# The last layer of a filter network on halves of TensorE's rows, two channel groups at a time

## The chip, the cores and the metric

The kernel runs on one core of a Trainium2 chip. The metric is the device time of one execution in microseconds; the median of several runs counts. An execution of the kernel before is shown by a hardware profile, on whose rows the text rests.

## The reference, cut to what matters

The program computes two layers of a hybrid network for 128 context tokens and 1024 latent tokens. Layer 0 has a state-space mixer and a Hyena mixer side by side, layer 1 is neighbourhood attention. The Hyena mixer convolves each of 1024 channels with a long filter that a small network computes from positions. Only this network is touched by the change:

```python
hdn = jnp.sin(freq * (feats @ w1 + b1))
hdn = jnp.sin(freq * (hdn @ w2 + b2))        # (L, 64)
filt = (hdn @ w3).astype(f32)                # w3: (64, 2048)
decay = jnp.exp(-t * jnp.abs(deltas)[None])
h_fwd = filt[:, :D_B] * decay
h_bwd = filt[:, D_B:] * decay
return jnp.concatenate([h_fwd, jnp.zeros((1, D_B), f32), h_bwd[:0:-1]], axis=0)
```

The last product, `hdn @ w3`, contracts over 64 hidden units only. It is needed for two directions (forward and backward), for a length of 1024 and one of 128, and for 8 groups of 128 channels. Its result times the decay is the filter, which the kernel then carries into the frequency domain.

## The kernel before, in words

The kernel is written with tiles, for which a framework derives the semaphores. It gives out buffers, and decides the order of each engine's instructions when the program is built; on the chip each engine then takes its own queue in that order. In the trace it can be seen that this order follows the program's text where work is ready, and takes later work forward where it isn't.

The projections set the frame. `proj` (L150 to L168) computes one chunk of 128 output channels for 1152 tokens as three blocks of 384 columns, each 24 matmuls on TensorE: 8 pieces of the inner dimension by three products (L160, L161, L162). The three products come from splitting each operand into a high and a low float32r part, hi·hi, hi·lo and lo·hi. Blocks go to a PSUM pool of three banks (`pj`); ScalarE empties them. Weights come by SP's queue into `wraw` one chunk ahead (`w_load`, L119), ScalarE casts the high part (`whi`, L132) and VectorE subtracts the low part (`wlo`, L133).

Between blocks, `tick` (L92) lets background work take a step: a Python generator runs up to its next `yield`, and what it issues stands between two blocks in the program's text. In the stage `xbc` (12 chunks, three ticks each, of which the first two chunks were computed ahead into three `pj` and three background banks) the one background generator is `filter_groups` (L526 to L569), at one step a tick. All background work takes its PSUM from a second pool of five banks (`bg`, `ps()`, L79).

`filter_groups` walks over the 8 channel groups. For each group it needs the filter in time, F (128 partitions, 18 blocks of 128 channels: 8 forward, 8 backward, 2 for the short length), which `filter_time` (L488 to L524) makes. Then come the first stage of a transform on VectorE (`stage_a`, L419, which starts with L537), the matmuls of the short transform (L548, L550) and of the second stage (`stage_b`, L464, lines L471 to L480), copies by ScalarE into H, and a store of H by the POOL queue. `filter_time` of the next group is called between `stage_a` and `stage_b` of this one, so F has two buffers.

`filter_time` for one group does the following.

- It fills a tile w3 of 128 rows and 256 columns: rows 0 to 63 hold the forward weights in columns 0 to 127, rows 64 to 127 the backward weights in columns 128 to 255, and the other two quarters are set to zero on POOL (L496, L497). ScalarE casts the high part wh (L500) and VectorE subtracts the low part wl (L501).
- The hidden layer `hdn` (high `hh`, low `hl`) has 128 partitions: 64 hidden units at the forward positions, and 64 at the backward ones. With the zeros in w3, one matmul over 128 rows gives both directions side by side.
- For each of 9 blocks j of 128 positions it issues three matmuls (L514, L515, L516) of 256 columns. Two j share one PSUM bank.
- ScalarE computes the decay with four exponentials of 128 by 128 (L519) into dc, which has one buffer. VectorE multiplies bank and dc into F (L520), one instruction of 512 columns for two j. The bank is free then.
- At last VectorE adds the bias row to position 0 (L523). Decay rates and bias come in one broadcast load, dl.

Of the kernel before, what the change touches and what calls it, by code (L numbers as in the profile page):

```python
# [9 lines left out]
AF = mybir.ActivationFunctionType  # L10
ALU = mybir.AluOpType
# [32 lines left out]
def bc(ap, shape):  # L44
    return ap.to_broadcast(shape)


class Net:
# [330 lines left out]
    def filter_mlp(self, keep, pool, px):  # L379
# [6 lines left out]
        for h in range(2):  # L386
            self.dma(w2[64 * h:64 * h + 64], i["hw2"])
        ft = self.t(pool, [128, 2304], "F", bufs=2)[0:33]
        self.dma(ft, i["feats"])
# [98 lines left out]
    def filter_time(self, g, pool):  # L488

        nc = self.nc  # L490
        i = self.i

        w3 = self.t(pool, [128, 256], "w3")
        wh = self.t(pool, [128, 256], "w3h", F32R)
        wl = self.t(pool, [128, 256], "w3l", F32R)
        nc.gpsimd.memset(w3[0:64, 128:256], 0.0)  # L496
        nc.gpsimd.memset(w3[64:128, 0:128], 0.0)  # L497
        for h in range(2):
            self.dma(w3[64 * h:64 * h + 64, 128 * h:128 * h + 128], i["hw3"][:, g, h])
        nc.scalar.copy(wh, w3)  # L500
        nc.vector.tensor_tensor(out=wl, in0=w3, in1=wh.bitcast(F32), op=ALU.subtract)  # L501
        dl = self.t(pool, [128, 2, 128], "dl")
        self.dma(dl.rearrange("p a c -> p (a c)"), i["dlhb"][g:g + 1].to_broadcast([128, 256]))
        F = self.t(pool, [128, 18, 128], "F", bufs=2)
        Fj = F[:, 0:16].rearrange("p (d j) c -> p j d c", d=2)
        hh, hl = self.hdn
        for j0 in range(0, 9, 2):
            n = min(2, 9 - j0)
            p = self.ps()
            dc = self.t(pool, [128, 2, 2, 128], "dc")  # L510
            for j in range(j0, j0 + n):
                o = p[:, (j - j0) * 256:(j - j0) * 256 + 256]
                js = slice(j * 128, j * 128 + 128)
                nc.tensor.matmul(o, hh[:, js], wh, start=True, stop=False)  # L514
                nc.tensor.matmul(o, hl[:, js], wh, start=False, stop=False)  # L515
                nc.tensor.matmul(o, hh[:, js], wl, start=False, stop=True)  # L516
                for d in range(2):
                    n1 = 8 * d + j if j < 8 else 16 + d
                    nc.scalar.activation(dc[:, j - j0, d], dl[:, 0], AF.Exp, scale=self.tcol[:, n1:n1 + 1])  # L519
            nc.vector.tensor_tensor(out=Fj[:, j0:j0 + 2] if n == 2 else F[:, 16:18].unsqueeze(1),  # L520
                                    in0=p[:, :n * 256].rearrange("p (j d c) -> p j d c", j=n, d=2), in1=dc[:, :n], op=ALU.mult)

        nc.vector.tensor_tensor(out=F[0:1, 0:17:16], in0=F[0:1, 0:17:16], in1=bc(dl[0:1, 1:2], [1, 2, 128]), op=ALU.add)  # L523
        return F  # L524

    def filter_groups(self, pool):  # L526

        nc = self.nc
        V = nc.vector
        self.tcol = self.t(pool, [128, 18], "tcol")  # L530
        self.dma(self.tcol, self.i["tcol"])
        Fn = self.filter_time(0, pool)
        yield
        for g in range(8):
            F = Fn
            sm = self.t(pool, [128, 8, 128], "sm")
            V.tensor_tensor(out=sm, in0=F[:, 0:8], in1=F[:, 8:16], op=ALU.add)  # L537
            V.tensor_tensor(out=F[:, 0:8], in0=F[:, 0:8], in1=F[:, 8:16], op=ALU.subtract)
            A = self.t(pool, [128, 16, 128], "A")
            self.stage_a(sm, F[:, 0:8], F[:, 8:10], F[:, 10:12], A, pool, "u8")  # L540
            yield
            if g < 7:
                Fn = self.filter_time(g + 1, pool)
                yield
            H = self.t(pool, [128, 20, 128], "H")
            p = self.ps()
            for n in range(2):
                nc.tensor.matmul(p[:, 0:128], self.tcf[:, n, :], F[:, 16 + n], start=(n == 0), stop=(n == 1))  # L548
            for n in range(2):
                nc.tensor.matmul(p[:, 128:256], self.tcf[:, 2 + n, :], F[:, 16 + n], start=(n == 0), stop=(n == 1))  # L550
            nc.scalar.copy(H[:, 18:20], p[:, 0:256].rearrange("p (a c) -> p a c", c=128))
            nc.scalar.copy(H[:, 17], p[:, 0:128])
            for k2 in range(4):
                p = self.ps()
                for j in range(2):
                    self.stage_b(A, 2 * k2 + j, p[:, j * 128:(j + 1) * 128], p[:, 256 + j * 128:256 + (j + 1) * 128])
                nc.scalar.copy(H[:, 1 + 2 * k2:3 + 2 * k2], p[:, 0:256].rearrange("p (a c) -> p a c", c=128))
                nc.scalar.copy(H[:, 9 + 2 * k2:11 + 2 * k2], p[:, 256:512].rearrange("p (a c) -> p a c", c=128))
                if k2 == 0:
                    nc.scalar.copy(H[:, 0], p[:, 0:128])  # L560
                if k2 == 1:
                    yield

            for b, im in ((0, 9), (17, 19)):
                V.tensor_copy(H[0:1, b], H[0:1, im])
                V.memset(H[0:1, im], 0.0)
            self.store(self.Hd[g], H)
            yield
# [1273 lines left out]
```

## Time and profile before

| | us |
|---|---|
| three runs | 2075.86, 2077.14, 2079.71 |
| median | 2077.14 |
| the profiled execution's own time | 2079.07 |
| its span, from the first to the last instruction | 2077.3 |
| TensorE matmuls busy in it | 2019.4 |
| VectorE busy | 1313.7 |
| ScalarE busy | 917.9 |

In the profile PE is TensorE's matmul queue, PEld its weight loads, DVE VectorE, ACT ScalarE, POOL GpSimd and SP the queue that issues most transfers. A row of the timeline gives the start in us, the duration, the engine, the line of the kernel, the operation, the tiles (written <- read), the shape and how many instructions were put together (x2). A shape such as 64*128 means a matmul over 64 rows of the array and 128 columns of weights; 128x256 is what streams through. Matmuls overlap, so the cost of one in a queue is the distance between the starts of two, not its duration.

### The profile page before, as it was taken

The numbers are of one execution on the slowest core, as the hardware profiler recorded it, in microseconds if no ns is written. First come the engines' busy times: TensorE is split into PE (matmuls) and PEld (weight loads), VectorE is DVE, ScalarE is ACT, GpSimd is POOL, SyncE is SP. The second block draws the span as 40 slices with busy tenths as digits, with TensorE's granted clock in tenths as the row PEclk, the third lists the DMA queues.
The fourth block names the chain that finished last, engine by engine and source line by source line (L and its number), as shares of the span: only waits on it lengthen the run. The fifth ranks groups of instructions, "written<-read, shape, count | busy, mean of one in ns | idle before, by whom it ended". The sixth has DMA issues, their size and how long they took to land.

```text
span 2077.3 us, 33946 instructions
## 1 busy us (share of the span) xinstructions
PE 2019.4 (97%) x13088; PEld 1820.7 (88%) x13088; DVE 1313.7 (63%) x2720; ACT 917.9 (44%) x2100; POOL 110.5 (5%) x233
## 2 busy tenths in 40 slices
PE   5999999999999999999999999999999999999998
PEld 3999997889999999888888899998888888888877
DVE  6887745145778787898899774654444344454464
ACT  3676642263333322554466511535445454443232
POOL 0010001110000000000000000100000000000000
PEclk9999999999999999999999999999999999999999
DMA  8142349554222113433353351422333223333462
GB/s 340 47 150 93 107 166 295 206 181 163 80 74 72 65 58 102 152 120 127 117 180 109 129 167 41 120 81 86 95 115 88 78 79 97 111 117 123 129 212 82
DMA packets 114265, 257.13 MB, mean 124 GB/s; under 512 B 27031, under 2 KB 62487, under 8 KB 111639
## 3 DMA queue, kind: packets, MB, share of 16 engines
q1 hardware_dynamic: 98728, 191.87, 29.1%
q0 software_dynamic: 15376, 63.09, 8.3%
q8 instruction: 104, 1.70, 0.4%
q14 instruction: 57, 0.47, 0.1%
HBM read 187.10 MB, written 67.80 MB: 123 GB/s over the span
## 4 chain that ended last, share of the span: by engine, by line
PE 82%; DVE 7%; DMA 4%; ACT 3%; issue 3%; SPq 0%; POOL 0%; POOLq 0%; DVEq 0%; ACTq 0%
PE pj L160 15%; PE pj L161 15%; PE pj L162 15%; PE bg L1315 3%; PE bg L1327 3%; PE bg L1298 3%; PE pj L1155 2%; PE pj L1156 2%; PE pj L1157 2%; PE bg L778 1%; PE bg L777 1%; PE bg L915 1%; PE pj L1353 1%; PE bg L290 1%; PE pj L1354 1%
## 5 line engine op out<-in xcount | busy, mean ns | idle before, releaser
L160 PE MATMUL pj<-hh,whi 128*128 128x384 f32 x1728 | 601.1, 348 | 2.7 <-DVE acc L846 1.8
L161 PE MATMUL pj<-hl,whi 128*128 128x384 f32 x1728 | 586.4, 339 | 0.0
L162 PE MATMUL pj<-hh,wlo 128*128 128x384 f32 x1728 | 586.1, 340 | 0.0
L160 PEld LDWEIGHTS pj<-hh,whi 128*128 128x128 f32 x1728 | 324.7, 188 | 23.7 <-issue 18.0
L161 PEld LDWEIGHTS pj<-hl,whi 128*128 128x128 f32 x1728 | 324.9, 188 | 7.5 <-issue 6.6
L162 PEld LDWEIGHTS pj<-hh,wlo 128*128 128x128 f32 x1728 | 324.6, 188 | 5.5 <-issue 4.5
L133 DVE TENSOR_TENSOR wlo<-wraw,whi 128x1024 fp32r<-128x1024 f32 x108 | 131.7, 1221 | 156.0 <-ACT whi L132 153.3
L132 ACT CAST whi<-wraw 128x1024 fp32r<-128x1024 f32 x108 | 113.3, 1050 | 259.1 <-PE pj L161 229.6
L1233 DVE CUSTOM_DVE_ANT_0 sz<-bg,Tb 128x512 f32<-128x512 f32 x128 | 83.5, 688 | 127.3 <-PE bg L1298 126.7
L583 ACT COPY raw<-pj 128x384 f32<-128x384 f32 (+2 forms) x140 | 56.0, 402 | 171.2 <-PE pj L162 84.0
L1235 ACT ACTIVATE sz<-sz,mx 128x512 f32<-128x512 f32 x128 | 91.6, 717 | 54.0 <-DVE mx L1233 53.2
L160 PE MATMUL pj<-yhi,whi 128*128 128x384 f32 x324 | 111.4, 344 | 3.8 <-DVE x L1076 2.8
L162 PE MATMUL pj<-yhi,wlo 128*128 128x384 f32 x324 | 110.8, 342 | 0.0
L161 PE MATMUL pj<-ylo,whi 128*128 128x384 f32 x324 | 109.7, 339 | 0.0
L1329 ACT COPY Pt<-bg 128x512 f32<-128x512 f32 (+1 forms) x144 | 71.9, 548 | 32.1 <-PE bg L1327 28.3
L1155 PE MATMUL pj<-whi,hh 128*128 128x256 f32 x288 | 82.9, 289 | 0.0
L1156 PE MATMUL pj<-wlo,hh 128*128 128x256 f32 x288 | 80.8, 281 | 0.0
L1157 PE MATMUL pj<-whi,hl 128*128 128x256 f32 x288 | 80.5, 280 | 0.0
L1327 PE MATMUL bg<-csq,sz 128*128 128x128 f32 x528 | 73.9, 280 | 0.0
L908 ACT ACTIVATE xw<-xt,wd 128x64 f32<-128x64 f32 x256 | 64.6, 336 | 8.7 <-PE bg L915 8.1
L1327 PEld LDWEIGHTS bg<-csq,sz 128*128 128x128 f32 x528 | 56.7, 141 | 13.0 <-issue 12.7
L160 PEld LDWEIGHTS pj<-yhi,whi 128*128 128x128 f32 x324 | 61.4, 189 | 7.1 <-issue 5.5
(411 smaller groups left out, 4021.3 us busy)
## 6 DMA issues: line engine op xcount, KB each, us to landing
wraw<-in_we SPq DMA_DIRECT2D x52, 512.0 KB, 3.6
wa<-in_wada SPq DMA_DIRECT2D x32, 512.0 KB, 6.8
wraw<-in_wo SPq DMA_DIRECT2D x24, 512.0 KB, 3.6
Tb<-Cd SPq DMA_DIRECT2D x256, 48.0 KB, 2.0
Hd<-H POOLq DMA_DIRECT2D x8, 1280.0 KB, 5.4
H<-Hd SPq DMA_DIRECT2D x8, 1280.0 KB, 6.5
xt<-xtd SPq DMA_DIRECT2D x17, 512.0 KB, 4.5
wraw<-in_woe SPq DMA_DIRECT2D x16, 512.0 KB, 4.2
```

The costliest lines, as they stand in the source:

```text
L132: self.nc.scalar.copy(hi, r)
L133: self.nc.vector.tensor_tensor(out=lo, in0=r, in1=hi.bitcast(F32), op=ALU.subtract)
L160: nc.tensor.matmul(p[:, :NB], wh, xh[k][:, sl], start=(k == 0), stop=False)
L161: nc.tensor.matmul(p[:, :NB], wh, xl[k][:, sl], start=False, stop=False)
L162: nc.tensor.matmul(p[:, :NB], wl, xh[k][:, sl], start=False, stop=(k == nk - 1))
L1155: nc.tensor.matmul(p[:, :256], self.hh[k][:, ts], hi[:, q:q + 256], start=(k == 0), stop=False)
L1156: nc.tensor.matmul(p[:, :256], self.hh[k][:, ts], lo[:, q:q + 256], start=False, stop=False)
L1157: nc.tensor.matmul(p[:, :256], self.hl[k][:, ts], hi[:, q:q + 256], start=False, stop=(k == 7))
L1233: V.tensor_tensor_reduce(out=z[:, :n], in0=s, in1=tb, scale=-1.0, scalar=3.0e38, op0=ALU.add, op1=ALU.min, accum_out=m1)
L1235: nc.scalar.activation(z[:, :n], z[:, :n], AF.Exp, bias=m1, scale=-1.0, accum_out=sm)
L1327: nc.tensor.transpose(pt[:, b * 128:(b + 1) * 128], p[:, b * 128:(b + 1) * 128], self.ident)
L1329: nc.scalar.copy(t[:, :nb * 128], pt[:, :nb * 128])
```

## The change

`filter_time` makes two groups at a time, and the two directions are no longer held apart by zeros.

- w3 now holds, in rows 0 to 63, the forward weights of both groups side by side (256 columns), and in rows 64 to 127 the backward weights of both. There are no zeros, and no memsets.
- Each matmul over 128 rows becomes two over 64: rows 0 to 63 (forward) into one PSUM bank, rows 64 to 127 (backward) into another. The two stand next to each other in the text. The columns stay 256, but they are now two groups of one direction, where they were two directions of one group. So a pair of groups has 54 matmuls of half height, where two calls before had 54 of full height.
- A block of two j takes two banks of the five.
- The multiply into F is done for each group and direction by itself: four instructions of 256 columns for a block of two j and two groups, where there were two of 512. dc is taken once for each group.
- The decay rates come in two loads, one for each group, and the two bias rows in two loads into a tile hb, which shares w3's buffer.
- `filter_groups` calls it before group 0 and again in groups 1, 3 and 5, behind the short transform's matmuls, where both F tiles have been read. The calls of the other groups and their yields fall away, so the generator has 28 yields where it had 32.

```diff
-        w3 = self.t(pool, [128, 256], "w3")
+        w3 = self.t(pool, [128, 2, 128], "w3")
...
-        nc.gpsimd.memset(w3[0:64, 128:256], 0.0)
-        nc.gpsimd.memset(w3[64:128, 0:128], 0.0)
         for h in range(2):
-            self.dma(w3[64 * h:64 * h + 64, 128 * h:128 * h + 128], i["hw3"][:, g, h])
+            self.dma(w3[64 * h:64 * h + 64], i["hw3"][:, g:g + 2, h])
...
+        hb = self.t(pool, [128, 2, 128], "w3")
+        for m in range(2):
+            self.dma(dl[:, m], i["dlhb"][g + m:g + m + 1, 0:128].to_broadcast([128, 128]))
+            self.dma(hb[0:1, m], i["dlhb"][g + m:g + m + 1, 128:256])
+        Fs = [self.t(pool, [128, 18, 128], "F", bufs=2) for n in range(2)]
         hh, hl = self.hdn
+        R = (slice(0, 64), slice(64, 128))
         for j0 in range(0, 9, 2):
             n = min(2, 9 - j0)
-            p = self.ps()
+            ps = [self.ps(), self.ps()]
             for j in range(j0, j0 + n):
-                nc.tensor.matmul(o, hh[:, js], wh, start=True, stop=False)
-                nc.tensor.matmul(o, hl[:, js], wh, start=False, stop=False)
-                nc.tensor.matmul(o, hh[:, js], wl, start=False, stop=True)
...
+                for x, w, st, sp in ((hh, wh, True, False), (hl, wh, False, False), (hh, wl, False, True)):
+                    for r, p in zip(R, ps):
+                        nc.tensor.matmul(p[:, o], x[r, js], w[r], start=st, stop=sp)
+            for m, F in enumerate(Fs):
+                dc = self.t(pool, [128, 2, 2, 128], "dc")
+                for d, p in enumerate(ps):
+                    n1 = 8 * d + j0 if j0 < 8 else 16 + d
+                    for j in range(n):
+                        nc.scalar.activation(dc[:, d, j], dl[:, m], AF.Exp, scale=self.tcol[:, n1 + j:n1 + j + 1])
+                    nc.vector.tensor_tensor(out=F[:, n1:n1 + n], in0=p[:, :n * 256].rearrange("p (j g c) -> p g j c", j=n, g=2)[:, m],
+                                            in1=dc[:, d, :n], op=ALU.mult)
...
         for g in range(8):
-            F = Fn
+            F = Fs[g % 2]
...
-            if g < 7:
-                Fn = self.filter_time(g + 1, pool)
-                yield
...
             nc.scalar.copy(H[:, 17], p[:, 0:128])
+            if g in (1, 3, 5):
+                Fs = self.filter_time(g + 1, pool)
+                yield
```

More of the change, by code (lines that the diff above doesn't have):

```diff
@@ L491, in filter_time @@
         i = self.i
-        w3 = self.t(pool, [128, 256], "w3")
+        w3 = self.t(pool, [128, 2, 128], "w3")
         wh = self.t(pool, [128, 256], "w3h", F32R)
         wl = self.t(pool, [128, 256], "w3l", F32R)
-        nc.gpsimd.memset(w3[0:64, 128:256], 0.0)
-        nc.gpsimd.memset(w3[64:128, 0:128], 0.0)
         for h in range(2):
-            self.dma(w3[64 * h:64 * h + 64, 128 * h:128 * h + 128], i["hw3"][:, g, h])
+            self.dma(w3[64 * h:64 * h + 64], i["hw3"][:, g:g + 2, h])
+        w3 = w3.rearrange("p a c -> p (a c)")
         nc.scalar.copy(wh, w3)
@@ L502, in filter_time @@
         dl = self.t(pool, [128, 2, 128], "dl")
-        self.dma(dl.rearrange("p a c -> p (a c)"), i["dlhb"][g:g + 1].to_broadcast([128, 256]))
-        F = self.t(pool, [128, 18, 128], "F", bufs=2)
-        Fj = F[:, 0:16].rearrange("p (d j) c -> p j d c", d=2)
+        hb = self.t(pool, [128, 2, 128], "w3")
+        for m in range(2):
+            self.dma(dl[:, m], i["dlhb"][g + m:g + m + 1, 0:128].to_broadcast([128, 128]))
+            self.dma(hb[0:1, m], i["dlhb"][g + m:g + m + 1, 128:256])
@@ L506, in filter_time @@
+        Fs = [self.t(pool, [128, 18, 128], "F", bufs=2) for n in range(2)]
         hh, hl = self.hdn
+        R = (slice(0, 64), slice(64, 128))
         for j0 in range(0, 9, 2):
             n = min(2, 9 - j0)
-            p = self.ps()
-            dc = self.t(pool, [128, 2, 2, 128], "dc")
+            ps = [self.ps(), self.ps()]
             for j in range(j0, j0 + n):
-                o = p[:, (j - j0) * 256:(j - j0) * 256 + 256]
                 js = slice(j * 128, j * 128 + 128)
[L514 to L524, printed above, removed]
+                o = slice((j - j0) * 256, (j - j0) * 256 + 256)
+                for x, w, st, sp in ((hh, wh, True, False), (hl, wh, False, False), (hh, wl, False, True)):
+                    for r, p in zip(R, ps):
+                        nc.tensor.matmul(p[:, o], x[r, js], w[r], start=st, stop=sp)
@@ L526, in filter_groups @@
+        for m, F in enumerate(Fs):
+            nc.vector.tensor_tensor(out=F[0:1, 0:17:16], in0=F[0:1, 0:17:16], in1=bc(hb[0:1, m:m + 1], [1, 2, 128]), op=ALU.add)
+        return Fs
     def filter_groups(self, pool):
@@ L531, in filter_groups @@
         self.dma(self.tcol, self.i["tcol"])
-        Fn = self.filter_time(0, pool)
+        Fs = self.filter_time(0, pool)
         yield
         for g in range(8):
-            F = Fn
+            F = Fs[g % 2]
             sm = self.t(pool, [128, 8, 128], "sm")
```

## Prediction

> **What bounds the kernel now.** I read the page first: the busy shares, the slices, the chain that ended last.
>
> ```profile
> span 2077.3 us, 33946 instructions
> ...
> PE 2019.4 (97%) x13088; PEld 1820.7 (88%) x13088; DVE 1313.7 (63%) x2720; ACT 917.9 (44%) x2100; POOL 110.5 (5%) x233
> ...
> PE   5999999999999999999999999999999999999998
> ...
> PE 82%; DVE 7%; DMA 4%; ACT 3%; issue 3%; SPq 0%; POOL 0%; POOLq 0%; DVEq 0%; ACTq 0%
> ```
>
> PE is busy 97% of the span and carries 82% of the chain. The filter network's last layer runs at about 70 to 255 us, as background work between the projections, so I took that stage alone: the busy time of each engine there (PE, PEld, DVE, ACT, POOL in this order, then granted clock, DMA share, GB/s), and what PE's matmuls waited for.
>
> ```profile
> 60.00:300.00 240.00, 237.41 (x1678) 230.75 (x1677) 182.98 (x350) 151.17 (x394) 23.42 (x61) 1.00 0.30 104
> ...
> 95.00:140.00 45.00, 42.85 (x318) 40.90 (x317) 41.79 (x92) 32.87 (x92) 7.28 (x17) 1.00 0.32 107
> ```
>
> ```profile
> PE bg L679 <- DVE F L520: 0.8, 1, 0.8
> ...
> PE pj L160 <- ACT acc L584: 0.6, 1, 0.6
> ```
>
> PE is without work for 2.6 of 240 us at full granted clock, and nearly all of that falls in 95 to 140 us, where DVE is busy 41.79 of 45 us. So here time is PE work: what the change takes out of PE's queue comes off the end, and what it puts in is added. The few waits are the ones that this stage makes: a PSUM bank not yet read out by the F multiply (L520), a projection bank not yet emptied.
>
> **What the layer costs now.** The groups of its lines in that window (name, shape, count, busy us, mean ns, idle before), then one whole call as PE runs it.
>
> ```profile
> L519 ACT ACTIVATE dc<-dl,tcol 128x128 f32<-128x128 f32 x144 | 46.9, 395 | 22.9 <-DMA dl<-in_dlhb 11.4 <-DVE F L520 11.4
> ...
> L520 DVE TENSOR_TENSOR F<-bg,dc 128x512 f32<-128x512 f32 x32 | 21.9, 685 | 17.5 <-PE bg L516 8.7 <-ACT dc L519 8.6
> ...
> L514 PE MATMUL bg<-w3h,hdh 128*128 128x256 f32 x72 | 20.7, 287 | 0.0
> L515 PE MATMUL bg<-w3h,hdl 128*128 128x256 f32 x72 | 20.2, 281 | 0.0
> L516 PE MATMUL bg<-w3l,hdh 128*128 128x256 f32 x72 | 20.2, 281 | 0.0
> ...
> L520 DVE TENSOR_TENSOR F<-bg,dc 128x256 f32<-128x256 f32 x8 | 3.4, 421 | 4.1 <-ACT dc L519 4.1
> ...
> L454 DVE SCALAR_TENSOR_TENSOR u<-u,u 128x128 f32<-128x128 f32 x8 | 2.3, 284 | 3.2 <-ACT u L438 3.2
> ...
> L496 POOL MEMSET w<- 64x128 f32 x7 | 1.4, 202 | 89.0 <-DVE w3l L501 60.0 <-ACT H L558 14.6 <-ACT dc L519 14.4
> ```
>
> ```profile
> 189.54 0.34 PE L162 MATMUL pj<-hh,wlo 128*128 128x384 f32 x1
> 189.72 0.28 PE L514 MATMUL bg<-w3h,hdh 128*128 128x256 f32 x1
> 189.84 0.28 PE L515 MATMUL bg<-w3h,hdl 128*128 128x256 f32 x1
> ...
> 192.80 0.28 PE L516 MATMUL bg<-w3l,hdh 128*128 128x256 f32 x1
> 192.92 0.34 PE L160 MATMUL pj<-hh,whi 128*128 128x384 f32 x1
> ```
>
> The mean of 281 ns is no price, since matmuls overlap; the distance between starts is. A call's 27 matmuls hold PE from 189.72 to 192.92: 3.20 us, or 0.119 each. Eight calls make 216 matmuls and 25.6 us; a pair of groups costs 6.4 us. A projection matmul steps by 0.18 us (L162 to L514).
>
> **What a pair on row halves costs.** The changed lines are not in this trace, but the attention (L1298) already issues float32r matmuls in pairs on rows 0 to 63 and 64 to 127, into two banks.
>
> ```profile
> 1508.80 0.28 PE L1156 MATMUL pj<-wlo,hh 128*128 128x256 f32 x1
> 1508.91 0.28 PE L1157 MATMUL pj<-whi,hl 128*128 128x256 f32 x1
> 1509.12 0.50 PE L1298 MATMUL bg<-KH,QH 64*128 64x512 f32 x2
> 1509.46 0.40 PE L1298 MATMUL bg<-KL,QH 64*128 64x512 f32 x2
> 1509.70 0.40 PE L1298 MATMUL bg<-KH,QL 64*128 64x512 f32 x2
> 1510.02 0.39 PE L1155 MATMUL pj<-whi,hh 128*128 128x256 f32 x1
> 1510.25 0.28 PE L1156 MATMUL pj<-wlo,hh 128*128 128x256 f32 x1
> 1510.37 0.28 PE L1157 MATMUL pj<-whi,hl 128*128 128x256 f32 x1
> ```
>
> Both halves of a pair start together (x2), and the pairs in the middle step by 0.24 us for 512 columns. So two half-height matmuls take the time of one full one. For 256 columns the bounds are 0.12 (half of 0.24) and 0.24 (no gain from fewer columns); I take 0.119, the full matmul of the same width, because 0.24 is twice that. The rows also show a price. L1157 to the first pair is 0.21 where L1156 to L1157 is 0.11; the first pair steps by 0.34 instead of 0.24; the last leaves after 0.32 instead of 0.24; the first full matmul behind it takes 0.23 instead of 0.12. Each change between full height and halves costs 0.10 + 0.10, an excursion in and out 0.40 us. [...]
>
> **The sum.** The number of matmuls stays: 216, now half as high. With p pairs, s matmuls left alone and e excursions, a pair of groups costs 0.119 x (p + s) + 0.40 x e against 6.4. What p, s and e become is decided by PSUM. A block of two j used one bank; now it uses two, so the five blocks of a call want ten, where the background pool has five. How the build orders PE's queue when a bank is missing is seen in the second call, while the first projections still hold three of the five:
>
> ```profile
> 91.34 0.28 PE L516 MATMUL bg<-w3l,hdh 128*128 128x256 f32 x1
> 91.46 0.34 PE L161 MATMUL pj<-hl,whi 128*128 128x384 f32 x1
> 91.63 0.34 PE L162 MATMUL pj<-hh,wlo 128*128 128x384 f32 x1
> 91.81 0.28 PE L514 MATMUL bg<-w3h,hdh 128*128 128x256 f32 x1
> ```
>
> The six matmuls of a block go in when its bank is free, and projection matmuls fill until the next: the order is by what is ready, instruction by instruction. The banks now come free at the pace of the exponentials and the multiply:
>
> ```profile
> 222.87 0.69 DVE L520 TENSOR_TENSOR F<-bg,dc 128x512 f32<-128x512 f32 x1 [1.35 <-ACT dc L519]
> 224.91 0.69 DVE L520 TENSOR_TENSOR F<-bg,dc 128x512 f32<-128x512 f32 x1 [0.80 <-ACT dc L519]
> ```
>
> ```profile
> 225.64 1.28 ACT L519 ACTIVATE dc<-dl,tcol 128x128 f32<-128x128 f32 x4 [0.76 <-DVE F L520]
> ```
>
> One turn is four exponentials (1.28) and a multiply (0.69), 2.04 us, because dc has one buffer. After the change a block of two j takes two turns, one for each group, of 1.28 + 0.42 + 0.07 = 1.77 us, and its banks are free only in the second: the first bank at about 2.8 us, the other two exponentials (0.64 us) later. PE would want them after 12 pairs, 1.4 us. So blocks one and two run in pairs on four banks, and from the third on each bank comes alone: its six half-height matmuls are ready while their partners, on the other bank, are not. I expect the pairs to break there.
>
> For each of the three later calls: 12 pairs and 30 alone, 42 x 0.119 = 5.0 us; excursions at least four (six alone take 0.71, which bridges the 0.64 between two banks of a block), at most six (each bank by itself): 1.6 to 2.4. That is 6.6 to 7.4 against 6.4, +0.2 to +1.0 each, +0.6 to +3.0 together. The first call has two banks: 6 pairs and 42 alone, 5.7 us, and five to nine excursions, 2.0 to 3.6: 7.7 to 9.3, +1.3 to +2.9. Together +1.9 to +5.9 us. I take +3, nearer to the lower end because of the bridging.
>
> The rest I cost at nothing on the path. DVE: 40 multiplies become 80, 64 x 0.421 + 16 x 0.284 = 31.5 against 25.3, +6.2 us; four of the eight casts and subtracts of w3 go. PE's queue covers this, 183 us of DVE work in 240; without the cover, at 95 to 140 us, a call's share of 6.2 / 4 = 1.6 us could show. ACT's 144 exponentials stay. The sixteen POOL memsets of 0.2 us go; behind them stood stores that PE does not wait for. On SP, six transfers for two groups stay six, but the hb rows take w3's buffer and so wait for the cast on ACT and the subtract on DVE; behind them queue the second dl, the second hb and the next weight loads, which whi and wlo wait for. A weight load has a whole chunk of 72 projection matmuls ahead, 72 x 0.18 = 13 us, to land; past that, PE would wait. The next w3 waits for the bias add, in time by a group. Four background steps fewer only move the work. F of a pair is ready after about 16 us (eight turns of 1.77 and two shorter), not 9, and its transforms start later, with projections to fill.
>
> Forecast: the profiled execution's 2079.07 us (span 2077.3) lies 1.9 above the median of the three runs, 2077.14; the difference goes onto the median: 2077.14 + 3 = 2080 us. By the cases' 1.9 to 5.9 its own range is 2079 to 2083.
>
> **Rivals.**
> *The pairs hold* (0.28): both banks of a block are handed out together. Then 27 x 0.119 = 3.2 us a call and four excursions, five in the first: 3 x (3.2 + 1.6 - 6.4) + (3.2 + 2.0 - 6.4) = -6.0, 2071 us. For it: every sextet of L1298 stays whole; against: none of them had to wait for a bank.
> *One excursion a call* (0.07): ordering leaves a call whole, 4 x (3.2 + 0.4 - 6.4) = -11.2, 2066 us. Against: ten banks from five. [...]
> *PE waits in its queue* (0.12): the order is fixed at build time, and PE takes its queue in order. If ACT and DVE empty the banks later than that order assumes, PE stands at a half-height matmul with projections behind it. Four waits a call of 0.8 us (the L679 wait) make 12.8 on top of little change without them: taken at half, +6.4 over the forecast, 2087 us. It decides from 0.1 us a wait. Against: the waits quoted hold one of this kind, 0.8 us.
> *The halves do not overlap at 256 columns* (0.03): no saving, 21 excursions x 0.4 = +8.4, 2086 us.
>
> **How the numbers follow.** The forecast has 0.50. A difference of 0.2%, 4.2 us, is about what a measurement of this kernel can tell: 2073 to 2081.3 is no change. Of the forecast's half, 0.30 lies within and 0.18 above, 0.02 below. Of the held pairs' 0.28, 0.20 are faster and 0.08 within. One excursion is faster (0.07), the last two slower (0.15, of which 0.02 within). That gives, rounded, faster 0.30, same 0.39, slower 0.31. The range from 2068 to 2088 leaves out most of the one-excursion case and half of PE's waits.
>
> **What would show it.** In the changed trace: pairs as x2 with starts 0.12 apart; runs of six 64*128 matmuls on one bank between projections; 4 to 9 excursions a call, each 0.40 over its matmuls' steps; the F multiply 80 times, at 0.42 us. Wrong: whole calls in x2 (the rivals above), a middle pair step near 0.24, or new PE waits on L520's successor of more than 2 us in sum.

## The result, and the profile after

| | median us | runs | ratio to before | 95% interval |
|---|---|---|---|---|
| before | 2077.42 | 2075.86 to 2079.71 | | |
| changed | 2102.89 | 2095.48 to 2105.07 | 1.0108 | 1.0089 to 1.0126 |

The change makes the kernel slower by 25 us, 1.1%. The forecast was 2080, the range ended at 2088. Medians and readings, here and below, leave out the four executions that took 2743 to 5041 us, among them the profiled one of the kernel with a late start. In the changed kernel the layer's matmuls are L517, its exponentials L523, the multiplies L524 and the bias add L528; the short transform is L550 and L552, the transposes of the convolution L684. The page of its profiled execution (2105.07 us, against 2079.07 before) shows the first trace of the loss:

```profile
span 2103.3 us, 33957 instructions
...
PE 2030.0 (97%) x13088; PEld 1822.8 (87%) x13088; DVE 1316.1 (63%) x2756; ACT 918.0 (44%) x2096; POOL 107.7 (5%) x217
...
PEclk9989999999999999999999999999999999999999
...
PE 62%; issue 21%; DVE 7%; DMA 5%; ACT 3%; POOL 1%; SPq 1%; POOLq 0%; DVEq 0%; ACTq 0%
```

PE has the same number of instructions and 10.6 us more busy time, because some of them ran slowly (a projection matmul steps by 0.32 us in 108.29 to 112.45, by 0.17 in 98.00 to 98.86): the granted clock falls in the third slice, which is the stage of the change. The stage by itself, and the part of it that the prediction quoted (same columns as there):

```profile
60.00:300.00 240.00, 225.54 (x1574) 211.59 (x1573) 176.86 (x381) 143.19 (x376) 19.54 (x44) 0.96 0.27 95
95.00:140.00 45.00, 36.53 (x246) 33.36 (x245) 37.89 (x86) 26.34 (x72) 3.67 (x7) 0.92 0.22 77
```

PE stands idle for 14.5 of 240 us where it was 2.6, and in 95 to 140 us it runs 246 matmuls where it ran 318. Over these 45 us DVE is not the cause by its amount of work: 37.89 us, against 41.79 before. It has less to do there, because it too gets its work later. What PE waited for in 60 to 320 us (sum, times, longest):

```profile
PE bg L517 <- DVE F L524: 5.0, 4, 2.6
PE bg L550 <- ACT raw L702: 3.0, 1, 3.0
PE pj L160 <- ACT acc L589: 1.9, 1, 1.9
PE bg L477 <- DVE F L524: 1.9, 1, 1.9
PE bg L471 <- DVE A L443: 1.8, 1, 1.8
```

Two kinds lie here. L517 waits for banks, as one rival had it. But the other four waits, 8.6 us, are by matmuls of other steps, which the prediction did not look at. The first of them, in the order of time:

```profile
101.47 0.34 PE L162 MATMUL pj<-hh,wlo 128*128 128x384 f32 x1
104.78 0.68 PE L550 MATMUL bg<-F,tcf 128*128 128x128 f32 x4 [2.98 <-ACT raw L702]
```

```profile
102.74 1.23 DVE L133 TENSOR_TENSOR wlo<-wraw,whi 128x1024 fp32r<-128x1024 f32 x1 [0.82 <-ACT whi L132]
103.88 0.48 DVE L524 TENSOR_TENSOR F<-bg,dc 128x128 f32<-128x128 f32 x2
104.28 0.40 DVE L528 TENSOR_TENSOR F<-F,w 1x256 f32<-1x256 f32 x1
```

In PE's queue the short transform of group 0 stands ahead of the next projections. It needs F of group 0. That is finished by the bias add at 104.28 + 0.40, and 0.1 us later PE goes on; the releaser that the row names, an ACT instruction, is only the last of several. That the add comes so late has to do with the queues too. The last exponentials of this F stand in ScalarE's queue behind the cast of the next chunk's weights (L132), and the cast waits 2.10 us for the running chunk's last L161; DVE's multiply stands behind `wlo` in the same way:

```profile
101.66 1.04 ACT L132 CAST whi<-wraw 128x1024 fp32r<-128x1024 f32 x1 [2.10 <-PE pj L161]
102.61 0.69 ACT L523 ACTIVATE dc<-dl,tcol 128x128 f32<-128x128 f32 x2
```

So in this order of the queues F could not be ready before PE had used up the projections that stand ahead of the short transform. Before, the same bias add stood much earlier:

```profile
90.51 0.41 DVE L523 TENSOR_TENSOR F<-F,dl 1x256 f32<-1x256 f32 x1
```

From the layer's first matmul (73.80 before, 74.61 after) to this add, 17 us have become 30. Behind the two places where waits of PE lie close together stands a stretch at half clock; behind the single wait of L471, 1.8 us at 204.8, there is none. The windows around the two (PE's busy time is the second number, the granted clock the third from the end):

```profile
102.50:105.90 3.40, 1.11 (x8) 0.97 (x8) 3.16 (x6) 2.55 (x6) 0.00 (x0) 1.00 0.25 64
105.90:112.70 6.80, 4.91 (x16) 4.90 (x16) 6.80 (x17) 5.71 (x16) 1.56 (x3) 0.50 0.50 171
136.60:140.00 3.40, 0.94 (x9) 0.77 (x9) 2.54 (x6) 3.40 (x11) 1.55 (x3) 1.00 0.40 118
140.00:150.30 10.30, 7.90 (x37) 7.11 (x38) 5.72 (x16) 5.22 (x18) 0.00 (x0) 0.50 0.25 73
```

PE was busy for a third of the 3.4 us ahead, and then for 6.8 and 10.3 us got half its clock. Close to the waits the engines that it waits for have little room: DVE (the fourth number) is busy for 3.16 of 3.40 us in the first window, ScalarE (the fifth) for all 3.40 in the third.

The loss can now be divided up. I take the distances between the starts of PE's successive instructions, sort them by kind, and count time beyond the end of an instruction as waiting, and half of PE's working time at half clock as clock loss (an estimate, by the steps of 0.32 and 0.17 us). Between two landmarks that both kernels have (the 121st projection matmul, and the first L290 behind the stage) this gives (differences of the unrounded values):

| us | before | after | difference |
|---|---|---|---|
| the layer's matmuls | 25.2 | 21.6 | -3.7 |
| projection matmuls (with the way out of each excursion) | 137.5 | 139.5 | +2.1 |
| other matmuls | 75.9 | 76.2 | +0.3 |
| waiting | 2.6 | 16.6 | +14.0 |
| half clock | 0 | 6.5 | +6.5 |
| the stretch | 241.2 | 260.3 | +19.2 |

Ahead of it 1.0 us is lost; behind it 3.1 in the next stage (a wait of 2.0 us at L684 and two more stretches of 3.4 us at half clock), and 2.7 up to the end: together the 26.0 us between the two executions. So the work on PE did become less. The loss is waiting, and the clock that waiting costs.

### The profile page after: what moved, and what is told of

The parts are those of the page before. It is cut to its first block, busy times and chain, and to the rows that moved or that the text cites. A ratio compares the mean times of both kernels' runs of the same rounds, so it can differ in the third digit from the quotient of the medians.

```text
span 2103.3 us, 33957 instructions
## 1 busy us (share of the span) xinstructions
PE 2030.0 (97%) x13088; PEld 1822.8 (87%) x13088; DVE 1316.1 (63%) x2756; ACT 918.0 (44%) x2096; POOL 107.7 (5%) x217
## 4 chain that ended last, share of the span: by engine, by line
PE 62%; issue 21%; DVE 7%; DMA 5%; ACT 3%; POOL 1%; SPq 1%; POOLq 0%; DVEq 0%; ACTq 0%
PE pj L160 12%; PE pj L161 12%; PE pj L162 12%; PE bg L783 1%; PE bg L782 1%; PE bg L920 1%; PE bg L995 1%; PE bg L290 1%; PE bg L477 1%; PE bg L478 1%; PE bg L479 1%; PE bg L480 1%; PE pj L1359 1%; PE pj L1358 1%; PE pj L1357 1%
## 5 line engine op out<-in xcount | busy, mean ns | idle before, releaser
L160 PE MATMUL pj<-hh,whi 128*128 128x384 f32 x1728 | 603.9, 349 | 3.8 <-ACT acc L589 1.9
L161 PE MATMUL pj<-hl,whi 128*128 128x384 f32 x1728 | 590.0, 341 | 0.0
L160 PEld LDWEIGHTS pj<-hh,whi 128*128 128x128 f32 x1728 | 326.8, 189 | 25.5 <-issue 17.8
L161 PEld LDWEIGHTS pj<-hl,whi 128*128 128x128 f32 x1728 | 326.8, 189 | 9.3 <-issue 7.3
L132 ACT CAST whi<-wraw 128x1024 fp32r<-128x1024 f32 x108 | 113.2, 1049 | 252.3 <-PE pj L161 229.4
L160 PE MATMUL pj<-yhi,whi 128*128 128x384 f32 x324 | 111.5, 344 | 3.8 <-DVE x L1081 2.8
L161 PE MATMUL pj<-ylo,whi 128*128 128x384 f32 x324 | 109.6, 338 | 0.0
L1332 PEld LDWEIGHTS bg<-csq,sz 128*128 128x128 f32 x528 | 56.7, 141 | 13.0 <-issue 12.8
L160 PEld LDWEIGHTS pj<-yhi,whi 128*128 128x128 f32 x324 | 61.4, 189 | 7.0 <-issue 4.5
```

What stands on the lines that cost most here:

```text
L132: self.nc.scalar.copy(hi, r)
L160: nc.tensor.matmul(p[:, :NB], wh, xh[k][:, sl], start=(k == 0), stop=False)
L161: nc.tensor.matmul(p[:, :NB], wh, xl[k][:, sl], start=False, stop=False)
L1332: nc.tensor.transpose(pt[:, b * 128:(b + 1) * 128], p[:, b * 128:(b + 1) * 128], self.ident)
```

## Experiments

The theory after the result: it is not the halves, it is that two groups are asked for at once, so F and its banks come late in an order that is fixed. The rivals: the halves' broken pairs and their changes to full height and back; the multiplies and exponentials of a pair, which hold banks longer.

**Are the halves the cause?** The matmuls of the changed kernel over all 128 rows, everything else the same. Both directions are summed in this filter, so it is not the reference's.

```diff
-                        nc.tensor.matmul(p[:, o], x[r, js], w[r], start=st, stop=sp)
+                        nc.tensor.matmul(p[:, o], x[:, js], w, start=st, stop=sp)
```

> The changed kernel with each matmul of the layer over all 128 rows again, same operands, columns, banks, order of calls and multiplies (both directions are summed into both banks, so the filter is not the reference's). Theory of the waits (PE stands in its queue for banks, F and A that two groups at once make late, and the clock drops behind these pauses): the matmuls cost 2 to 4 us more, the pauses stay near the 16.6 us of the changed kernel and stretches at half clock appear in the stage, 2095 to 2110 us. Rival of the halves (the change of tiling and the half-filled array cost the time and the clock): full clock in the stage, 2076 to 2084 us.

2102.71 us, ratio 1.0117 (1.0096 to 1.0138): level with the changed kernel. By the division above, the layer's matmuls take 25.7 us and the projections 137.0, so the halves were worth 4.2 - 2.5 = 1.7 us of PE's work, and waiting and clock (14.1 and 8.0 us here, 16.6 and 6.5 there) took 0.9 of it back; the rest is within the measurement. Its waits are the same ones:

```profile
PE bg L517 <- DVE F L524: 3.4, 2, 2.2
PE bg L550 <- ACT raw L702: 3.0, 1, 3.0
```

**A shorter turn.** dc in two halves, so that exponentials of one direction run beside the multiply of the other.

```diff
-                dc = self.t(pool, [128, 2, 2, 128], "dc")
                 for d, p in enumerate(ps):
+                    dc = self.t(pool, [128, 2, 128], "dc", bufs=2)
```

> The changed kernel with dc cut into two tiles of half the size, one for each direction, in two buffers, so that exponentials need not wait for the multiply. Theory of the waits: a turn falls from 1.77 us to the 1.28 us of its four exponentials, banks and F come a quarter earlier, and 8 to 15 us come back, 2088 to 2096 us, with fewer PE pauses on the F multiply. Rival of the halves: no more than 4 us of difference, 2098 to 2106 us.

2102.8 us, 1.011 (1.008 to 1.0139): no gain, where the theory had expected 8 to 15 us. The wait of the short transform is gone, and two others take its place: 4.3 us by stage_b (L471) for the first stage of group 0's transform, and 4.0 by the layer's matmuls for a bank that ScalarE empties. The chain is only late one step further on.

**One group at a time, on halves.** Weights of one group, 128 columns, four j to a bank, so six banks a call, in the old order of the calls.

```diff
-        for j0 in range(0, 9, 2):
-            n = min(2, 9 - j0)
+        for j0 in range(0, 9, 4):
+            n = min(4, 9 - j0)
```

> The kernel before with matmuls on row halves, but for one group at a time and in the old order of calls: weights of 128 columns, a bank for each direction with four j in it, six banks a call instead of five. Theory of the waits: no lumps, PE pauses in the stage stay below 6 us and the clock stays full; 27 pairs of some 0.11 us a call save little, two or three excursions of 0.4 us a call cost 6 to 10 us: 2076 to 2087 us. Rival of the halves: half-clock stretches appear here too and the time is above 2090 us.

2115.25 us, 1.0178 (1.0159 to 1.0196), the slowest of all, where I had hoped for a level result. A block now holds its banks for eight exponentials in a row, and PE waits for them seven times, 17 us, and 44 us are at half clock (mean clock 0.985 in its profiled execution, 0.989 in the changed kernel's):

```profile
PE bg L513 <- DVE F L519: 17.0, 7, 3.4
```

It also has twice the number of matmul instructions, so it says that banks matter, not what two groups at once cost.

**Two groups at once, nothing else.** The kernel before, with its own full-height matmuls, multiply and one bank a block; only the calls for two groups stand together, at the changed kernel's places.

```diff
-        Fn = self.filter_time(0, pool)
+        Fs = [self.filter_time(n, pool) for n in range(2)]
...
-            if g < 7:
-                Fn = self.filter_time(g + 1, pool)
-                yield
...
             nc.scalar.copy(H[:, 17], p[:, 0:128])
+            if g in (1, 3, 5):
+                Fs = [self.filter_time(g + 1 + n, pool) for n in range(2)]
+                yield
```

> The kernel before with full-height matmuls, one bank for two j and the wide multiply, but two calls back to back, for groups 0 and 1, and again in groups 1, 3 and 5 as in the changed kernel. Theory of the waits, if two groups at once and the later call are enough: PE pauses of 8 us or more, half clock, 2090 to 2105 us. If the doubled banks of a block are what it takes: 2077 to 2085 us. Rival of the halves: 2077 to 2081 us.

2100.54 us, 1.0105 (1.0086 to 1.0124). This is 23 of the 25 us without any of the change's instructions. Its waits are another pair, of 2.7 and 5.0 us between 113 and 128 us, with half clock behind them:

```profile
PE bg L471 <- DVE F L520: 5.2, 2, 5.0
PE bg L514 <- DVE F L520: 2.7, 1, 2.7
```

So the order of the calls is enough for a loss of this size, and neither rival is needed for it. The waits are not at the changed kernel's places, though, and here VectorE has little room: in 107 to 128 us it is busy for 19.8 of 21 us.

```profile
107.00:128.00 21.00, 13.18 (x80) 11.75 (x78) 19.80 (x42) 12.53 (x39) 2.82 (x8) 0.78 0.31 110
```

**Spreading a call.** Two more yields inside each call, behind the second and behind the fourth block; the same with full height (directions summed, not the reference's filter); the same with dc in halves; and the same number of yields behind each call instead of in it.

```diff
+            if j0 in (2, 6):
+                yield
         for m, F in enumerate(Fs):
...
-        Fs = self.filter_time(0, pool)
+        Fs = yield from self.filter_time(0, pool)
```

> The changed kernel with two more yields in each call, behind the second and the fourth block, so that three steps share a call and projections stand between them (36 yields as there are 36 ticks, where the changed kernel has 28). Theory of the waits, now: PE's queue asks for banks, F and A before they are there, since the steps stand too close. Then PE pauses in the stage fall from 16.6 to under 6 us, hardly any half clock is left, and most pairs hold: 2070 to 2084 us. Rival of the lump (two groups at once are too much work for ACT and DVE wherever the steps stand): pauses above 10 us, 2090 to 2105 us.

> The same as e5_spread with the layer's matmuls over all 128 rows (both directions summed into both banks, not the reference's filter). What row halves are worth without the pauses: by the price of pairs in the prediction, 27 pairs and three excursions a call, 3.2 + 1.2 against 6.4 us, this one is 4 to 8 us slower than e5_spread; if pairs break at the banks even so, 0 to 3 us. Theory of the waits: 2075 to 2090 us; rival of the lump: above 2090 us.

> e5_spread with dc in two half tiles as in e2_dc_halves. Theory of the waits: the turn is no longer what is late, so within 3 us of e5_spread. Rival of the lump: the shorter turn gives back 5 us or more.

> The changed kernel with the same number of yields as e5_spread, but all behind the call (three instead of one), so that the call's five blocks stay in one step and only what uses F comes later. If the lateness of F and A is what costs: near e5_spread, 2072 to 2086 us. If the waits for banks inside the call cost as much: half way, 2084 to 2096 us.

2095.87, 2095.62, 2091.99 and 2101.89 us (1.0087, 1.0077, 1.0067 and 1.0109; the last interval is 1.0095 to 1.0124). Spreading takes 7 us off the medians (for the second kernel the intervals lie apart, for the first they overlap), with dc in halves 11; yields behind a call take 1, which is within the interval. That is less than the theory had expected of each of them, 2070 to 2090 us: asking later gives a part back, not the whole. The first kernel's time and its 10.5 us of waiting are even what its rival had given, two groups at once as too much work for ScalarE and VectorE wherever the steps stand; the two kernels at the end of this section speak against that. Of the later waits one of 2.1 us is left in the first and in the fourth kernel. The wait of 3.0 us for group 0's F stays in the first, second and fourth, in the second as the only large one besides the bank behind it; in the third, 4.3 us by L471 take its place. The second kernel's:

```profile
PE bg L552 <- ACT raw L704: 3.0, 1, 3.0
PE pj L160 <- ACT acc L591: 1.9, 1, 1.9
```

With these yields, 8 more than the changed kernel, the stage ends later in the program's order, and the next stage's first matmuls wait for weights: L290 for `wa` three times, 2.0 us in sum, in the first kernel (325 to 380 us).

Between the first two, the halves save 3.1 us of matmuls (19.2 + 141.2 against 25.0 + 138.5), and PE waits 4.5 us longer (10.5 against 6.0). The times are level.

**A later start.** Fewer steps in the first three chunks, in the changed kernel; with dc in halves, one more yield in the later calls and 1.1 steps a tick behind the third chunk; that at full height (directions summed); and the two old calls together with the later start.

```diff
         for j in range(12):
+            self.rate = 0.34 if j < 3 else self.RX
```

> The changed kernel with the background steps held back in the first three chunks (one step a chunk instead of three), so that projections stand between the first call and what uses its F. If the pauses come from PE's queue asking too early, the first one (4.9 us at 101 to 108 us, and the half clock behind it) goes, the later ones may stay: 2085 to 2096 us. If the pair's work is too much in any order, the pause only moves: 2097 to 2106 us.

> e9_late_start with dc in two half tiles, one yield in each of the three later calls (behind the second block) and 1.1 steps a tick, so that the steps end in time. If the early asking is the cause: PE pauses in the stage below 6 us, little or no half clock, 2073 to 2087 us. If the lump is: above 2090 us.

> e10_late_spread with the layer's matmuls over all 128 rows (both directions summed into both banks, not the reference's filter): what row halves are worth where PE hardly pauses. In e5_spread against e6_spread_full they took about 3 us out of PE's own work; so this one is 1 to 6 us slower than e10_late_spread.

> e4_two_calls (full height, old multiply, two calls back to back) with the background steps held back in the first three chunks as in e9_late_start. If asking too early is what cost e4_two_calls its 23 us, half or more comes back: 2077 to 2090 us; if not, 2095 to 2103 us.

2097.27, 2105.21, 2099.64 and 2092.93 us (1.0098, 1.0124, 1.0098, 1.0072). A later start does not bring the time back. For the changed kernel the intervals with and without it overlap. The second kernel, expected at 2073 to 2087 us if early asking was the cause, came out above 2090, and the third was faster than the second, not slower. The two old calls gain 7.6 of their 23 us, with intervals that just overlap. The waits join into one, 12.3 us in the second kernel, 12.6 in the third and 7.5 in the fourth, where the convolution's transposes wait for VectorE. The second kernel's wait, and its window:

```profile
PE bg L686 <- DVE acc L706: 12.3, 1, 12.3
```

```profile
98.00:112.00 14.00, 1.78 (x11) 1.42 (x9) 14.00 (x30) 5.45 (x12) 0.99 (x1) 0.67 0.25 66
```

Here VectorE is the limit by its amount of work: it is busy without a gap from 98 to 112 us, with group 0's first stage ahead of the convolution. In the changed kernel itself it was not. The theory of a full VectorE, which some of my expectations name, holds for variants like this one; what all have in common is that the operands of the next matmul in PE's queue are late.

**Which of the calls?** The change was cut in two. In the first kernel groups 0 and 1 come from old one-group calls at their old places and 2 to 7 from pairs; the second is that at full height (directions summed); the third is the complement, a pair for 0 and 1 and old calls behind; the fourth is the first with a yield in each pair's call.

```diff
-        Fs = self.filter_time(0, pool)
+        Fs = [self.filter_one(0, pool)]
...
             yield
+            if g == 0:
+                Fs.append(self.filter_one(1, pool))
+                yield
             H = self.t(pool, [128, 20, 128], "H")
```

> Groups 0 and 1 get their F from two of the old one-group calls, where they stood before; groups 2 to 7 in pairs on halves of the rows, as in the changed kernel. If the loss lies in the first call (F of group 0 ready at about 104 us instead of 90 on a full VectorE): the waits of about 3 us for group 0's short transform and 1.9 us for a projection bank are gone, and with them the half clock of 105.9 to 112.7 us: 2083 to 2092 us. If it lies as much in the later calls: 2095 us or more, with half a dozen waits of the layer's matmuls for VectorE's multiplies left.

> The run before it with the pair's matmuls over all 128 rows, so that both directions are summed in the filter: its values are not the reference's. By the price of the halves (three quarters of the layer's matmuls saved at 0.24 us a step of two, less 0.4 us an excursion) this is 2 to 4 us slower than the run before it. If saved matmul time is given back as waits, as in the two spread kernels, the two agree within 1.5 us.

> The complement: groups 0 and 1 as one pair on halves of the rows, as in the changed kernel; groups 2 to 7 by the old one-group calls where they stood before. If the first call makes the loss, most of the 25 us stays: 2090 to 2102 us, with the waits of 3 and 1.9 us near 101 to 106 us and half clock behind them. If the later calls make it: 2082 us or less.

> As the first of these, and each later pair's call cut in two steps, so that its multiplies come in two lots. If the later calls' waits for multiplies are what is left, it is 2 to 5 us faster than the first of these, and level with the kernel before or a little ahead of it: 2074 to 2085 us. If a step more only delays the end of the filter's work and with it the next stage's weights, it is no faster than the first of these.

2091.91 us (1.006, 1.0046 to 1.0075), 2092.95 (1.0055, 1.0037 to 1.0072), 2091.81 (1.0059, 1.004 to 1.0078) and 2087.32 (1.0031, 1.0018 to 1.0044), against 2078.63. The loss splits evenly: 13.3 us without the first pair, 13.2 with it alone, and 26.5 is about the whole 25.5. So neither "the first call" nor "the later calls" is the cause alone; both parts cost. The fourth kernel, with a yield in each pair's call, is 4.6 us faster than the first, but not level with the kernel before, as its expectation had it. The third kernel shows the changed kernel's first two waits again:

```profile
PE bg L471 <- ACT H L595: 3.9, 2, 2.4
PE bg L591 <- ACT raw L740: 3.0, 1, 3.0
PE pj L160 <- ACT acc L627: 1.9, 1, 1.9
```

The first kernel has them no longer, but others, of which the second one here (L591 is its short transform) tells most:

```profile
PE bg L517 <- ACT H L595: 3.9, 1, 3.9
PE bg L591 <- DVE F L566: 2.7, 1, 2.7
```

```profile
104.96 0.39 PE L480 MATMUL bg<-A,tf 128*128 128x128 f32 x2
108.08 0.68 PE L591 MATMUL bg<-F,tcf 128*128 128x128 f32 x4 [2.73 <-DVE F L566]
```

Behind group 0's last stage_b (L480), group 1's short transform comes at once, and waits for group 1's F. In the kernel before, the call for group 2 stood behind that stage_b: 27 matmuls, 3.2 us, in which VectorE finished (110.04 + 0.41). A chunk of projections followed, and the short transform came only at 127.55:

```profile
107.61 0.36 PE L514 MATMUL bg<-w3h,hdh 128*128 128x256 f32 x1
110.04 0.41 DVE L523 TENSOR_TENSOR F<-F,dl 1x256 f32<-1x256 f32 x1
127.55 0.61 PE L548 MATMUL bg<-F,tcf 128*128 128x128 f32 x4
```

With pairs, no call stands between a group's stage_b and the next group's short transform; in every other group one stands behind the short transform instead. That gave a prediction.

**The place.** Groups 0, 1, 2 and 7 by old calls at their old places, so that the first 130 us have their fillers; only 3 with 4 and 5 with 6 as pairs, each with one yield in it (the edit is against the fourth kernel above); and the same with these two pairs at full height (directions summed, not the reference's filter).

```diff
-            F = Fs[g % 2]
+            F = Fs[g]
...
-            if g == 0:
-                Fs.append(self.filter_one(1, pool))
+            if g in (0, 1, 6):
+                Fs.append(self.filter_one(g + 1, pool))
                 yield
...
-            if g in (1, 3, 5):
-                Fs = yield from self.filter_time(g + 1, pool)
+            if g in (2, 4):
+                Fs += yield from self.filter_time(g + 1, pool)
```

> Groups 0, 1, 2 and 7 by the old one-group calls where they stood before, 3 with 4 and 5 with 6 as pairs on halves of the rows behind the short transforms of groups 2 and 4, each pair's call cut in two steps. If a pair costs because the one-group call that stood between a group's first step and its short transform is missing there (matmuls that filled TensorE while VectorE worked), then up to 130 us this runs as before: no wait over 1 us there, no half clock. The two pairs save about 2 x 2 us of matmuls and meet a VectorE that has room by then: 2074 to 2081 us, level with before. If a pair costs about 4 us wherever it stands: 2086 us or more, with waits of TensorE for multiplies in 130 to 230 us.

> The run before it with the two pairs' matmuls over all 128 rows, both directions summed, so that the filter's values are not the reference's. If the halves' saved matmul time reaches the end once waits are few, this is 2 to 5 us slower than the run before it; if it is given back as waits, the two agree within 1.5 us.

2084.02 us, 1.0027 (1.0014 to 1.0039), and 2080.63, 1.0003 (0.9992 to 1.0015), against 2079.6. The first 130 us now run as before: the 2.7 us wait is gone, none is above 0.9 (halves) or 1.1 us (full height), and there is no half clock. Two pairs for two groups at a time, at full height and in a stretch where VectorE has room, cost nothing that can be measured. The missing call alone costs nothing either: here too none stands ahead of the short transforms of groups 2 to 5. Group 2's, in the full-height kernel, follows group 1's stage_b at once and does not wait, since its F had been finished 5.9 us before:

```profile
130.86 0.41 DVE L568 TENSOR_TENSOR F<-F,dl 1x256 f32<-1x256 f32 x1
136.92 0.39 PE L480 MATMUL bg<-A,tf 128*128 128x128 f32 x2
137.15 0.61 PE L593 MATMUL bg<-F,tcf 128*128 128x128 f32 x4
```

So asking for two groups is not dear in itself; it is dear where F is late and the call that it takes away was the filler.

The halves, however, are 3.4 us slower than the full height here, the opposite of what the expectation gave them. The rows of the halves' kernel show why:

```profile
142.32 0.38 PE L517 MATMUL bg<-w3h,hdh 64*128 64x256 f32 x1 [1.56 <-ACT H L597]
...
145.74 0.52 PE L161 MATMUL pj<-hl,whi 128*128 128x384 f32 x1
146.06 0.52 PE L162 MATMUL pj<-hh,wlo 128*128 128x384 f32 x1
...
146.89 0.41 PE L517 MATMUL bg<-w3h,hdl 64*128 64x256 f32 x1
147.11 0.41 PE L517 MATMUL bg<-w3l,hdh 64*128 64x256 f32 x1
```

```profile
140.50:143.90 3.40, 1.84 (x11) 1.27 (x10) 2.65 (x4) 2.58 (x7) 0.00 (x0) 1.00 0.12 48
143.90:150.70 6.80, 6.80 (x24) 5.92 (x23) 4.58 (x11) 5.36 (x17) 1.56 (x3) 0.50 0.53 164
```

The full-height kernel in the same place:

```profile
137.00:157.00 20.00, 19.43 (x134) 18.47 (x135) 14.62 (x34) 13.37 (x37) 2.32 (x6) 1.00 0.35 128
```

With halves, PE is through the first two blocks sooner, and stands 1.56 us for a bank that ScalarE empties, where the full height stands 0.57 in the whole window. For the 6.8 us behind it PE has half clock: a projection matmul steps by 0.32 us (145.74 to 146.06) instead of 0.18, a half-height one by 0.22 (146.89 to 147.11) instead of 0.12. Divided up as above over the stretch, the halves save 3.5 us of the layer's matmuls and give back 1.1 at the projections, 2.6 as waits and 3.4 by the clock: a loss of 3.6 us, where the medians are 3.4 apart.

Halves against full height, with all else the same, over the five pairs of kernels (the changed one first): 2102.89 and 2102.71; spread, 2095.87 and 2095.62; late, 2105.21 and 2099.64; first calls old, 2091.91 and 2092.95; two pairs, 2084.02 and 2080.63. In none do the halves gain what can be measured. No version beats the kernel before. How the 13 us of the later pairs divide between the missing filler and the waits for banks was not taken apart, and no kernel was run that leaves the pairs where they are and moves only the short transforms behind the next projections.

## Why the prediction was wrong

- **PE is the bound, so its waiting shows at the end.** Right, and more so than the text used it: 14.0 us of waiting and 6.5 of clock in the stage are the loss.
- **The step of a pair, 0.119 us for 256 columns.** Right. In the last call of the changed kernel:

```profile
225.63 0.28 PE L517 MATMUL bg<-w3h,hdl 64*128 64x256 f32 x2
225.75 0.28 PE L517 MATMUL bg<-w3l,hdh 64*128 64x256 f32 x2
...
226.93 0.28 PE L517 MATMUL bg<-w3h,hdh 64*128 64x256 f32 x1
227.04 0.28 PE L517 MATMUL bg<-w3h,hdl 64*128 64x256 f32 x1
```

- **Pairs break at the third block.** Right: twelve pairs in a row, then singles (x1), one bank after the other. Over the four calls 64 pairs ran side by side (starts under 0.07 us apart; 52 of them the two halves of one step, 12 of different steps) and 88 matmuls were alone, where the text had 42 and 132. There are 20 excursions, 8 in the first call and 4, 5 and 3 in the later ones, where it had 5 to 9 and 4 to 6.
- **The sum for the matmuls, +1.9 to +5.9 us.** Wrong by its sign: -1.6. More pairs held, and an excursion cost less than 0.40: 64 fewer steps of 0.119 are -7.6, so 20 excursions made 6.0, 0.30 each.
- **DVE +6.2 us, covered.** The size was a little high, 29.8 against 25.3, +4.5 us:

```profile
L524 DVE TENSOR_TENSOR F<-bg,dc 128x256 f32<-128x256 f32 x64 | 25.8, 419 | 17.8 <-ACT dc L523 16.5 <-PE bg L517 1.2
L524 DVE TENSOR_TENSOR F<-bg,dc 128x128 f32<-128x128 f32 x16 | 4.0, 282 | 0.2
```

  DVE's amount of work was not what cost time in the changed kernel (37.89 us against 41.79 in 95 to 140).
- **"F of a pair is ready after about 16 us ..., not 9, and its transforms start later, with projections to fill."** This is the step that failed, and it was costed at nothing. For the first call it was 30 us, and in the kernel before 17, not 9; for the later ones it was 23, 25 and 19, not 16. And the projections did not fill: PE's queue holds the short transform ahead of them, so it waits 2.98 us; ScalarE's copies of that bank come late, and the projections' own bank with them (L160, 1.9 us). The step "four background steps fewer only move the work" failed with it: the steps that fell away were the calls between one group's stage_b and the next group's short transform, which filled PE while VectorE worked. That restoring three of them takes the waits of the first 130 us away was shown by the last two kernels; that the change of the calls' order alone costs 23 us, by the two old calls put together.
- **The rival "PE waits in its queue".** This was the mechanism, given 0.12, and the text's own sign of it, waits on the multiplies of more than 2 us in sum, was there with 5.0. It looked only at waits for banks by the layer's own matmuls; these made 5.5 us, where 12.8 had been taken at half. The 8.6 us of other waits and the clock behind all of them were not in it, so even its 2087 us was too low.
- **Halves that do not overlap, pairs that hold, one excursion a call.** None of these came, and none could have decided: with the matmuls at full height the time is the same.
- **SP's queue and the weights.** As said: PE waited 0.2 us for wlo.

## What to carry to other kernels

A piece of background work on the bound engine can also be the filler that hides another engine's chain; before it is made cheaper or moved, look at what stands behind it in that engine's queue and when the operands of that are ready. Here the move cost 23 us where they were late, and nothing where they had been ready for 5.9. A saving in such a piece can turn into waiting: of the 3.5 us of matmuls that the halves saved with two pairs none reached the end, since 1.1 came back at the projections, 2.6 as waits and 3.4 by the clock. That it would come off the end if the next one's operands were early by as much is an estimate that no run showed. In these traces a wait of about 2 us on TensorE had to be priced with the half clock that could follow it: with two pairs, 1.6 us of waiting stood ahead of 6.8 us at half clock, which cost 3.4.

## What the runs showed of the hardware

- **The clock fell behind waits inside a busy stage.** The stretches at half clock in this stage are 3.4 to 23.9 us long; the changed kernel's are 6.827 (from 105.90 us) and 10.240 (from 140.03), two and three times the 3.413 that single ones last in the same trace (at 338.00 and 365.31). Cut into windows of that length on the grid of these changes, the profiled executions of the two kernels and of 17 experiments have 26 windows in 60 to 330 us in which PE had full clock and was idle for 0.55 of the window or more: behind each the clock was halved. With 0.44 to 0.54 it was halved behind 6 of 14, and with less behind 2 of 1394. In the changed kernel the two windows ahead of its half clock were idle for 0.67 and 0.72, and one at 201.47 us with 0.54 had full clock behind it; in the kernel with two pairs on halves PE was busy for 1.84 of 3.4 us and had half its clock in the next 6.8.
- **One kernel's time went with its clock.** The runs of the kernel with groups 0 and 1 by old calls and its pairs at full height lie at 2084.3 and 2085.6 us with a granted clock of 0.995 and 0.994, and at 2092.5 to 2094.6 with 0.989 to 0.992. From 0.995 to 0.990 it is 10.3 us (2084.3 and 2094.6). The whole span of the profiled execution has 48.4 us at half clock in the changed kernel (mean 0.989), and 20.1 in the kernel before (0.995).
- **An excursion to half height and back** cost 0.30 us on the mean of 20 in the changed kernel, an estimate from the sum of its matmuls (-1.6 us) and its 64 pairs, against 0.40 in the kernel before around the attention's sextet at 1508.80 to 1510.37 us.
